# A two-layer decoder step: the first half's output projection inside the second half's attention, and smaller first chunks in three feed forwards

## The chip, the cores and the metric

The kernel runs on one core of a Trainium2 chip, as one program in one launch. The metric is the device time of that launch in microseconds (us). Five engines take part, each with its own queue that is worked off in order: TensorE (PE in the profile, with its weight loads as PEld), VectorE (DVE), ScalarE (ACT), GpSimd (POOL) and SyncE (SP, which issues nearly all DMAs).

## What is computed

One inference step of a decoder of two layers, in float32, with a model width of 1024, for 512 tokens of a prompt and 8 x 4 new tokens of other sequences. Cut to what matters here:

```python
for l in range(2):
    x = x + swiglu_half(x, ffn1_norm[l], ffn1_w_gu[l], ffn1_w_down[l])
    h = rmsnorm(x, mix_norm[l])
    # layer 0: gated linear attention; layer 1: sliding window of 128 with sinks
    q, k, v, ..., mq = split(h @ w_in)
    tok = gla_chunked(...) if l == 0 else swa_prompt(...)
    mo = mem_attention(mq, mem_k[l], mem_v[l])      # 256 memory tokens
    x = x + concatenate([tok, mo]) @ w_out
    x = x + swiglu_half(x, ffn2_norm[l], ffn2_w_gu[l], ffn2_w_down[l])
y = rmsnorm(x, final_norm)

def swiglu_half(x, g, w_gu, w_down):
    gate, up = split(rmsnorm(x, g) @ w_gu, 2)
    return 0.5 * ((silu(gate) * up) @ w_down)       # inner width 2816
```

## The kernel before

**Tiles.** The residual stream stands transposed, 8 tiles of 128 channels, in two halves of the tokens: half 0 has 288 columns (256 of the prompt and the 32 new ones), half 1 has 256. Every float32 matmul of the dense layers is made of three products in the fp32r type, high by high, high by low and low by high. So every weight and every activation is split into two parts: the high one by a copy on ACT (L298), the low one by a subtraction on DVE (L299). Names like `g6l`, `u1l`, `d7l`, `op7l` are the low parts of a gate, up, down or output projection weight block, those with `h` the high parts, those with `r` the block as loaded.

**A feed forward** has an inner width of 2816, 22 blocks of 128. `CHUNKS` cuts them into three chunks: 8, 7 and 7. Chunk 0 is done by `ffn` (L552) in a plain form for each half apart: per block a gate and an up product of 8 x 3 matmuls each, then the down projection of the chunk, 8 output tiles, each with 3 matmuls per block, whose sum is added to the residual tile (L580). Chunks 1 and 2 are done by `ffn_pair` (L498) for both halves at once, which stand beside each other in 272 columns: gate and up of the two halves are a product of 2 x 2 blocks, and it is computed with 7 products instead of 8, each of 12 matmuls. For this, sums and differences of the weights are formed per block in `quads` (L315; `s6s`, `t6s` are sums of block 6, `s6l` the low part of such a sum) and sums of the activations once per feed forward in `pair` (L443). `ffn_pair` opens each chunk with two matmuls that only open its two banks (L510).

**The order of a layer** is written in `layer` (L1259). A half goes through chunk 0 of its own; the joint chunks stand between: (1) chunk 0 of ffn1 for half 0, from the layer before or the start; (2) `enter_pair`, the norm and the joint forms, then the joint chunks (`both`); (3) chunk 0 of ffn1 for half 1 (`late`); (4) the norm and input projection of half 0 (`enter`, `project`); (5) attention of half 0, into which `weave` mixes what is left of `late`, the norm of half 1 and its input projection; (6) the output projection of half 0 (`out_proj`, L749; its residual adds are L755), with `hold` units of half 1's input projection kept back and put behind it, beside the norm for ffn2 (`enter`: `rstd` L394, whose sums over the channels are L404 on PE and whose scaling `r` is L410 on DVE, and `normed` L432); (7) attention of half 1, into which chunk 0 of ffn2 for half 0 is mixed; (8) the output projection of half 1; (9) `enter_pair` and the joint chunks of ffn2, beside the rest of chunk 0. In layer 0 the projection of the second layer's memory keys (`late_mem`) stands between (6) and (7).

A unit is a piece of a generator that ends at a `yield`: a gate or an up product of one block, an output tile of a projection, a step of an attention. `weave` (L1325) takes units of its two generators in proportion to the numbers that it is given. `FILL` holds for each layer how many units go ahead of the first weave (`lead`), are put just behind it (`pad`), are kept back (`hold`), come behind the second weave (`last`) and are kept for the entry of the joint chunks (`more`). `EARLY` is the number of units of chunk 0, two for each block and 8 for the down projection, 24.

In layer 1 the attention of the window (`swa_prompt`, L1125) works in groups of two heads: scores on PE (L1134), masks and sums on DVE (L1150 to L1170), transposes on PE (L1172), copies on DVE (L1176), values on PE (L1142). The order in which the engines' queues are filled comes from a scheduler with priorities: chunk ends ask for 6000 (`AHEAD`), the norms for 6500 (`SOON`), the attention in a weave for 3000 (`LEAD`). Dense matmuls of the plain form and all down and other projections are recorded at L356, those of `ffn_pair` at L342.

Of the kernel before, what the change touches and what calls it, by code (L numbers as in the profile page):

```python
# [30 lines left out]
SC = slice(2 * P, 2 * P + NS)  # L31
FF = 2816
FT = FF // P
CHUNKS = ((0, 8), (8, 15), (15, 22))
PW = (2 * P + NS + 2 * P) // 2
HK = KD // 2
EARLY = 2 * CHUNKS[0][1] + KD
MT = 256
GH, GK, GV = 4, 96, 192
LEVELS = (64, 32, 16, 8, 4, 2, 1)  # L40
# [128 lines left out]
def take(gen, n):  # L169
    for _ in range(n):  # L170
        if next(gen, StopIteration) is StopIteration:
            return
        yield


def drain(*gens):
    for g in gens:
        for _ in g:
            pass
# [53 lines left out]
class Build:  # L233
# [1 line left out]
    WB = (3, 4, 4, 2)  # L235
    MIX = 10
    FIRST, AHEAD, SOON, LEAD = 20000, 6000, 6500, 3000
    FILL = ((6, 1, 7, 2, 6), (7, 2, 5, 0, 9))
    HOMES = ((13, 8, 3), (8, 8, 3))

    def __init__(self, ctx, tc, d):
# [258 lines left out]
    def ffn_pair(self, tag, c, xs, gathered=()):  # L500


        nc = self.nc
        gu, dn = self.d["gu_" + tag], self.d["dn_" + tag]
        f0, f1 = CHUNKS[c]
        xa = [(h[:, :PW], l[:, :PW]) for h, l in xs[0]]
        xb, (t1, t2, t3, t4) = xs[1], xs["forms"]
        ga, gb = [], []
        for bank in self.pb.banks:
            nc.tensor.matmul(bank[:, :PW], xa[0][0][:, :P], xa[0][0], start=True, stop=True, skip_group_check=True)  # L510
        for f in range(f0, f1):
            w1, w2, s1, s2, s3, s4, w4 = self.quads(gu, f)
            pa, pc, pb = (b()[:, :PW] for b in (self.pac, self.pac, self.pb))
            c5, c2, act = (self.gas.u(PW) for _ in range(3))
            ahead = lambda: self.tc.high_priority(offset=self.AHEAD)
            self.product(pa, w1, xa[:HK], True)
            with ahead():
                nc.scalar.activation(pb, pa, AF.Copy)
            self.product(pc, s1, t1, True)
            self.product(pb, s2, t2, False)  # L520
            with ahead():
                nc.scalar.activation(c5, pc, AF.Copy)
            self.product(pa, w2, xa[HK:], False)
            with ahead():
                nc.scalar.activation(c2, pb, AF.Copy)
            self.product(pb, s3, t3, False)
            with ahead():
                nc.scalar.activation(act, pa, AF.Silu)
                nc.vector.tensor_tensor(out=c5, in0=c5, in1=pb, op=ALU.add)
            self.product(pc, s4, xb[HK:], False)  # L530
            self.product(pb, w4, t4, False)
            with ahead():
                nc.vector.tensor_tensor(out=c2, in0=c2, in1=pc, op=ALU.add)  # L533
                nc.scalar.activation(c2, c2, AF.Silu)  # L534
                nc.vector.tensor_tensor(out=act, in0=act, in1=pb, op=ALU.mult)
                ga.append(self.split(act, PW))
                nc.vector.tensor_tensor(out=c2, in0=c2, in1=c5, op=ALU.mult)  # L537
                gb.append(self.split(c2, PW))
            yield
        for m in range(KD):  # L540
            po = self.dense(dn[m, :, f0:f1, :], [ga, gb], f"d{m}")
            x0, x1 = self.x[0][m], self.x[1][m]
            with self.tc.high_priority(offset=self.AHEAD):
                for x, p in ((x0[:, :PW], po[0]), (x0[:, PW:], po[1][:, NH[1]:]), (x1, po[1][:, :NH[1]])):
                    nc.vector.scalar_tensor_tensor(out=x, in0=p, scalar=0.5, in1=x, op0=ALU.mult, op1=ALU.add)  # L545
            for h in gathered:
                self.stats((x0, x1)[h], h)
            if m == KD - 1:
                self.drop(ga, gb)
            yield  # L550

    def ffn(self, tag, c, halves, xs, gathered=(), tanh=False):  # L552
        nc = self.nc
        gu, dn = self.d["gu_" + tag], self.d["dn_" + tag]
        f0, f1 = CHUNKS[c]
        gs = {h: [] for h in halves}
        parts = [[(a[:, :NH[h]], b[:, :NH[h]]) for a, b in xs[h]] for h in halves]
        for f in range(f0, f1):
            pg = self.dense(gu[f], parts, f"g{f}")
            act = [self.gas.u(NH[h]) for h in halves]  # L560
            with self.tc.high_priority(offset=self.AHEAD):
                for a, p in zip(act, pg):
                    if tanh:
                        nc.scalar.activation(a, p, AF.Tanh, scale=0.5)
                        nc.vector.scalar_tensor_tensor(out=a, in0=a, scalar=1.0, in1=p, op0=ALU.add, op1=ALU.mult)
                    else:
                        nc.scalar.activation(a, p, AF.Silu)
            yield
            pu = self.dense(gu[FT + f], parts, f"u{f}")
            with self.tc.high_priority(offset=self.AHEAD):  # L570
                for h, a, p in zip(halves, act, pu):
                    nc.vector.tensor_tensor(out=a, in0=a, in1=p, op=ALU.mult)
                    gs[h].append(self.split(a, NH[h]))
            yield
        for m in range(KD):
            po = self.dense(dn[m, :, f0:f1, :], [gs[h] for h in halves], f"d{m}")
            for i, h in enumerate(halves):
                x = self.x[h][m]
                with self.tc.high_priority(offset=self.AHEAD):
                    nc.vector.scalar_tensor_tensor(out=x, in0=po[i], scalar=0.25 if tanh else 0.5, in1=x,  # L580
                                                   op0=ALU.mult, op1=ALU.add)
                if h in gathered:
                    self.stats(x, h)
            if m == KD - 1:
                self.drop([gs[h] for h in halves])
            yield
# [680 lines left out]
    def layer(self, l, project, attend, w_out, xs):  # L1267
# [16 lines left out]
            self.drop(r)  # L1284

        def both(tag, xs):
            drain(self.ffn_pair(tag, 1, xs), self.ffn_pair(tag, 2, xs, gathered=(0,)))
            self.drop(xs[0], self.extra)

        lead, pad, hold, last, more = self.FILL[l]  # L1290
        both(f1, xs)
        late = self.ffn(f1, 0, (1,), xs, gathered=(1,), tanh=True)
        mix[0] = enter(0, f"mix_{l}")
# [6 lines left out]
            mix[1] = enter(1, f"mix_{l}")  # L1300
            yield from project(1, mix[1], s[1])

        fill, units = second(), EARLY - lead + (22 if l == 0 else 8) - hold - pad
        self.weave(attend(0, s[0]), (take(fill, units), units))
        drain(take(fill, pad))
        self.drop(s[0].q if l else [])
        drain(self.out_proj(w_out, s[0].toks + s[0].mo, 0))
        out[0] = enter(0, f"ffn2_{l}")
        drain(fill)
        if l == 0:  # L1310
            drain(self.late_mem())
        early = self.ffn(f2, 0, (0,), out, tanh=True)
        more += last
        self.weave(attend(1, s[1]), (take(early, EARLY - more), EARLY - more))
        drain(take(early, last))
        self.drop(s[1].q if l else [])
        drain(self.out_proj(w_out, s[1].toks + s[1].mo, 1))
# [188 lines left out]
```

## Time and profile before

| what | us |
|---|---|
| time, median of 3 runs | 2153.05 |
| lowest and highest of these | 2150.55, 2155.71 |
| the profiled execution: device time | 2148.32 |
| the profiled execution: span of the core | 2146.5 |
| TensorE busy in the span | 2065.4 |
| VectorE busy in the span | 1539.5 |
| ScalarE busy in the span | 1067.2 |

The span runs from the first to the last instruction that the profile shows, and the device time lies 1.8 us above it. Busy times are sums over the instructions of an engine, so two engines that are busy at the same time both count. The mean clock that TensorE was granted is 0.983 of full speed. Where a row has several times, the first is the start in the span, the second the length.

### The profile page before, as it was taken

The numbers are of one execution on the slowest core, as the hardware profiler recorded it, in microseconds if no ns is written. First come the engines' busy times: TensorE is split into PE (matmuls) and PEld (weight loads), VectorE is DVE, ScalarE is ACT, GpSimd is POOL, SyncE is SP. The second block draws the span as 40 slices with busy tenths as digits, with TensorE's granted clock in tenths as the row PEclk, the third lists the DMA queues.
The fourth block names the chain that finished last, engine by engine and source line by source line (L and its number), as shares of the span: only waits on it lengthen the run. The fifth ranks groups of instructions, "written<-read, shape, count | busy, mean of one in ns | idle before, by whom it ended". The sixth has DMA issues, their size and how long they took to land.

```text
span 2146.5 us, 41032 instructions
## 1 busy us (share of the span) xinstructions
PE 2065.4 (96%) x16428; PEld 2000.7 (93%) x16428; DVE 1539.5 (72%) x3234; ACT 1067.2 (50%) x2089; POOL 35.8 (2%) x69
## 2 busy tenths in 40 slices
PE   6999999999999998999999999999998999999998
PEld 6999999998799998999999999999986988999998
DVE  7876675576668869757587776665877877966655
ACT  5554444754646645535355553444544544544434
POOL 5000000000000000000000000000000000000000
PEclk9999999999999999999999999999998999999999
DMA  7533253434454342323354523243443434232344
GB/s 230 157 115 109 79 156 118 138 120 148 152 160 159 125 143 79 108 87 103 113 178 142 177 89 114 74 148 122 151 147 105 143 109 128 89 109 79 110 149 128
DMA packets 90496, 273.03 MB, mean 127 GB/s; under 512 B 11408, under 2 KB 25248, under 8 KB 90272
## 3 DMA queue, kind: packets, MB, share of 16 engines
q1 hardware_dynamic: 89728, 269.87, 39.8%
q8 instruction: 129, 2.11, 0.4%
q14 instruction: 63, 0.52, 0.1%
q10 hardware_dynamic: 576, 0.52, 0.1%
HBM read 264.04 MB, written 7.70 MB: 127 GB/s over the span
## 4 chain that ended last, share of the span: by engine, by line
PE 85%; DVE 8%; DMA 4%; ACT 2%; issue 2%; SPq 0%; DVEq 0%; ACTq 0%
PE bank L356 55%; PE bank L342 21%; PE bank L904 1%; PE bank L1142 1%; DVE u L299 1%; PE bank L1134 1%; DMA u19r<-gu_ffn 0%; PE bank L649 0%; DMA u21r<-gu_ffn 0%; DMA u20r<-gu_ffn 0%; PE bank L705 0%; PE bank L416 0%; PE bank L679 0%; PE bank L1030 0%; PE bank L668 0%
## 5 line engine op out<-in xcount | busy, mean ns | idle before, releaser
L298 ACT ACTIVATE u<-u 128x272 fp32r<-128x272 f32 (+3 forms) x328 | 134.0, 422 | 132.5 <-DVE u L537 55.2
L545 DVE SCALAR_TENSOR_TENSOR x<-bank,x 128x16 f32<-128x16 f32 (+2 forms) x192 | 59.7, 342 | 115.0 <-PE bank L356 114.2
L299 DVE TENSOR_TENSOR u<-u,u 128x272 fp32r<-128x272 f32 (+3 forms) x328 | 137.2, 429 | 3.0 <-ACT u L298 1.2
L356 PE MATMUL bank<-u,d0h 128*128 128x272 f32 (+2 forms) x352 | 71.3, 289 | 0.0
L356 PE MATMUL bank<-u,d1h 128*128 128x272 f32 (+2 forms) x352 | 70.3, 288 | 0.0
L356 PE MATMUL bank<-u,d2h 128*128 128x272 f32 (+2 forms) x352 | 68.6, 289 | 0.4 <-DVE x L755 0.4
L356 PE MATMUL bank<-u,d3h 128*128 128x272 f32 (+2 forms) x352 | 68.0, 290 | 0.0
L356 PE MATMUL bank<-u,d4h 128*128 128x272 f32 (+2 forms) x352 | 67.5, 289 | 0.0
L356 PE MATMUL bank<-u,d5h 128*128 128x272 f32 (+2 forms) x352 | 67.3, 289 | 0.0
L356 PE MATMUL bank<-u,d6h 128*128 128x272 f32 (+2 forms) x352 | 67.1, 288 | 0.0
L356 PE MATMUL bank<-u,d7h 128*128 128x272 f32 (+2 forms) x352 | 67.0, 288 | 0.0
L534 ACT ACTIVATE u<-u 128x272 f32<-128x272 f32 x56 | 24.1, 430 | 73.2 <-DVE u L533 73.2
L356 PEld LDWEIGHTS bank<-u,d0h 128*128 128x128 f32 x352 | 56.3, 188 | 0.2
L356 PEld LDWEIGHTS bank<-u,d2h 128*128 128x128 f32 x352 | 55.4, 188 | 0.9 <-issue 0.5
L356 PEld LDWEIGHTS bank<-u,d1h 128*128 128x128 f32 x352 | 56.1, 188 | 0.0
L356 PEld LDWEIGHTS bank<-u,d3h 128*128 128x128 f32 x352 | 55.3, 188 | 0.3 <-DVE x L580 0.3
L356 PEld LDWEIGHTS bank<-u,d4h 128*128 128x128 f32 x352 | 55.4, 188 | 0.0
L356 PEld LDWEIGHTS bank<-u,d5h 128*128 128x128 f32 x352 | 55.2, 188 | 0.1
L356 PEld LDWEIGHTS bank<-u,d6h 128*128 128x128 f32 x352 | 55.2, 188 | 0.0
L356 PEld LDWEIGHTS bank<-u,d7h 128*128 128x128 f32 x352 | 55.1, 188 | 0.1
L356 PE MATMUL bank<-u,d2l 128*128 128x272 f32 (+2 forms) x176 | 51.0, 290 | 0.0
L356 PE MATMUL bank<-u,d4l 128*128 128x272 f32 (+2 forms) x176 | 50.9, 289 | 0.0
(1178 smaller groups left out, 7664.7 us busy)
## 6 DMA issues: line engine op xcount, KB each, us to landing
g0r<-gu_ffn SPq DMA_DIRECT2D x8, 512.0 KB, 3.5
u0r<-gu_ffn SPq DMA_DIRECT2D x8, 512.0 KB, 3.4
g1r<-gu_ffn SPq DMA_DIRECT2D x8, 512.0 KB, 3.4
u1r<-gu_ffn SPq DMA_DIRECT2D x8, 512.0 KB, 3.5
g2r<-gu_ffn SPq DMA_DIRECT2D x8, 512.0 KB, 3.4
u2r<-gu_ffn SPq DMA_DIRECT2D x8, 512.0 KB, 3.9
g3r<-gu_ffn SPq DMA_DIRECT2D x8, 512.0 KB, 3.5
u3r<-gu_ffn SPq DMA_DIRECT2D x8, 512.0 KB, 3.6
```

Of the source, the lines that this page charges most:

```text
L298: nc.scalar.activation(h, src, AF.Copy)
L299: nc.vector.tensor_tensor(out=l, in0=src, in1=h.bitcast(F32), op=ALU.subtract)
L342: self.nc.tensor.matmul(ps, a[:, k, :], x, start=start and k == 0 and j == 0, stop=k == len(xs) - 1 and j == 2, skip_group_check=True)
L356: self.nc.tensor.matmul(ps, w[:, k, :], x, start=i == 0 and j == 0, stop=i == kc - 1 and j == 2)
L534: nc.scalar.activation(c2, c2, AF.Silu)
L545: nc.vector.scalar_tensor_tensor(out=x, in0=p, scalar=0.5, in1=x, op0=ALU.mult, op1=ALU.add)
L904: nc.tensor.matmul(pv[:, c * half:(c + 1) * half], lhs[:, c * P:(c + 1) * P], second(rhs[:, c * P:(c + 1) * P]), start=True, stop=True)
L1134: nc.tensor.matmul(ps[:, e, P * (1 - back):][:, :P], q[j][64 * half:64 * half + 64, cols], self.keys(kv, half, n - back), start=True, stop ...
L1142: nc.tensor.matmul(dst, self.vt[n - i][:, 64 * kv:64 * kv + 64], pt[i].rearrange("p g t -> p (g t)"), start=i == 0, stop=i == last)
```

## The change

It has two parts.

**Chunks.** `CHUNKS` becomes a table with a row for each feed forward. ffn1_1 keeps 8, 7 and 7 blocks; ffn1_0, ffn2_0 and ffn2_1 get four chunks, 6, 6, 5 and 5. So in these three, two blocks more go from the plain to the joint form, and there is one joint chunk more. `EARLY` is 20 for them.

**Weave.** The kept back units of half 1's input projection (`hold`) now follow the first attention at once, ahead of the output projection of half 0; `pad` is gone. The output projection, the norm behind it and chunk 0 of ffn2 (in layer 0 with `late_mem` ahead) become one generator, `third`, which is mixed into the attention of half 1. `FILL` has other numbers.

```diff
-CHUNKS = ((0, 8), (8, 15), (15, 22))
+SMALL, LARGE = ((0, 6), (6, 12), (12, 17), (17, 22)), ((0, 8), (8, 15), (15, 22))
+CHUNKS = {"ffn1_0": SMALL, "ffn2_0": SMALL, "ffn1_1": LARGE, "ffn2_1": SMALL}
-EARLY = 2 * CHUNKS[0][1] + KD
+EARLY = {tag: 2 * c[0][1] + KD for tag, c in CHUNKS.items()}
-    FILL = ((6, 1, 7, 2, 6), (7, 2, 5, 0, 9))
+    FILL = ((6, 8, 2, 8), (7, 5, 0, 10))
...
         def both(tag, xs):
-            drain(self.ffn_pair(tag, 1, xs), self.ffn_pair(tag, 2, xs, gathered=(0,)))
+            last = len(CHUNKS[tag]) - 1
+            drain(*(self.ffn_pair(tag, c, xs, gathered=(0,) if c == last else ()) for c in range(1, last + 1)))
...
-        lead, pad, hold, last, more = self.FILL[l]
+        lead, hold, last, more = self.FILL[l]
...
-        fill, units = second(), EARLY - lead + (22 if l == 0 else 8) - hold - pad
+        fill, units = second(), EARLY[f1] - lead + (22 if l == 0 else 8) - hold
         self.weave(attend(0, s[0]), (take(fill, units), units))
-        drain(take(fill, pad))
+        drain(fill)
         self.drop(s[0].q if l else [])
-        drain(self.out_proj(w_out, s[0].toks + s[0].mo, 0))
-        out[0] = enter(0, f"ffn2_{l}")
-        drain(fill)
-        if l == 0:
-            drain(self.late_mem())
-        early = self.ffn(f2, 0, (0,), out, tanh=True)
-        more += last
-        self.weave(attend(1, s[1]), (take(early, EARLY - more), EARLY - more))
+
+        def third():
+            if l == 0:
+                yield from self.late_mem()
+            yield from self.out_proj(w_out, s[0].toks + s[0].mo, 0)
+            out[0] = enter(0, f"ffn2_{l}")
+            yield from self.ffn(f2, 0, (0,), out, tanh=True)
+
+        early, units = third(), EARLY[f2] + KD + (6 if l == 0 else 0) - more - last
+        self.weave(attend(1, s[1]), (take(early, units), units))
```

In the changed kernel a line of code beyond the first stands one line lower (L299 is L300, L755 is L756).

How the queues change is shown at three places. The first is DVE's queue at the entry of the joint chunks of ffn1 in layer 0, where the last joint forms of the activations (`u_825`, `u_829`, of `pair`) and the first weight sums (`s8s`, `t8s`) are made. Before:

```order
L299 TENSOR_TENSOR u_825<-u_694,u_824 128x272
L299 TENSOR_TENSOR d6l<-d6r,d6h 128x1024
L299 TENSOR_TENSOR u_829<-u_695,u_828 128x272
L580 SCALAR_TENSOR_TENSOR x_117<-bank_68,x_117 128x288
L299 TENSOR_TENSOR d7l<-d7r,d7h 128x1024
L580 SCALAR_TENSOR_TENSOR x_119<-bank_69,x_119 128x288
L299 TENSOR_TENSOR g8l<-g8r,g8h 128x1024
L327 TENSOR_TENSOR s8s<-u8r 128x512
L330 TENSOR_TENSOR t8s<-g8r,u8r 128x512
L580 SCALAR_TENSOR_TENSOR x_121<-bank_67,x_121 128x288
L328 TENSOR_TENSOR s8s<-s8s,g8r 128x512
```

DVE at the same place in the changed kernel, where the first joint block is block 6:

```order
L300 TENSOR_TENSOR g6l<-g6r,g6h 128x1024
L328 TENSOR_TENSOR s6s<-u6r 128x512
L331 TENSOR_TENSOR t6s<-g6r,u6r 128x512
L481 TENSOR_TENSOR u_695<-u_695,u_331 128x272
L300 TENSOR_TENSOR u_825<-u_694,u_824 128x272
L581 SCALAR_TENSOR_TENSOR x_123<-bank_67,x_123 128x288
L581 SCALAR_TENSOR_TENSOR x_125<-bank_68,x_125 128x288
L329 TENSOR_TENSOR s6s<-s6s,g6r 128x512
L300 TENSOR_TENSOR u_829<-u_695,u_828 128x272
L332 TENSOR_TENSOR t6s<-g6r,s6s 128x512
L300 TENSOR_TENSOR s6l<-s6s,s6h 128x1024
```

The weight sums of the first joint block now stand among the last forms of `pair`, ahead of `u_825` and `u_829`, and all residual adds of chunk 0 (`x_123`, `x_125` are the last two) stand ahead of `s6l`; before, two of them stood further back.

The second place is DVE in layer 1 from the last residual add of half 0's output projection (`x_125`) on. `bmq0l` and `bmq1l` are weight blocks of half 1's input projection, L1046 to L1048 its rotary embedding, `r` the scaling of the norm's sums. Before:

```order
L755 TENSOR_TENSOR x_125<-x_125,bank_69 128x288
L299 TENSOR_TENSOR bmq0l<-bmq0r,bmq0h 128x1024
L1046 STREAM_SHUFFLE u_20187<-bank_69 128x256
L1047 TENSOR_TENSOR u_20188<-bank_69,u_19697 128x256
L1048 TENSOR_TENSOR u_20187<-u_20187,u_19699 128x256
L410 TENSOR_SCALAR r<-bank_67 128x2
```

In the changed kernel DVE's rows from the same add on begin so (L1156 to L1171 are masks and softmax of half 1's attention):

```order
L756 TENSOR_TENSOR x_125<-x_125,bank_69 128x288
L300 TENSOR_TENSOR u1l<-u1r,u1h 128x1024
L300 TENSOR_TENSOR u_20118<-bank_72,u_20117 128x128
L1156 COPY_PREDICATED bank_71<-masks,bank_71 128x2x128
L300 TENSOR_TENSOR u_20120<-bank_72,u_20119 128x128
L1156 COPY_PREDICATED bank_70<-masks,bank_70 128x2x128
L300 TENSOR_TENSOR u_20122<-bank_72,u_20121 128x128
L1159 TENSOR_REDUCE wx<-bank_70 128x2
```

DVE's queue in the changed kernel reaches the scaling `r` with these rows, the last two of which are the 41st and 42nd behind the add:

```order
L1162 TENSOR_SCALAR wx<-wx 128x2
L1169 RECIPROCAL ws<-ws 128x2
L1171 TENSOR_SCALAR u_20676<-u_20676,ws 128x128 x2
L411 TENSOR_SCALAR r<-bank_67 128x2
L411 TENSOR_SCALAR r<-bank_67 32x1
```

Before, weight splits and rotary steps of half 1's input projection stood between the add and `r`, 5 rows; in the changed kernel 40 rows stand there, most of them softmax steps of half 1's attention.

The third place is PE's queue in layer 1, behind the last matmuls of half 0's output projection (`op7`). `bq3` is a weight block of half 1's input projection; L404 are the norm's sums. Before:

```order
L356 MATMUL bank_69<-u_18167,op7h 128x288
L356 MATMUL bank_69<-u_18168,op7h 128x288
L356 MATMUL bank_69<-u_18167,op7l 128x288
L404 MATMUL bank_67<-ones,u_19843 128x1
L356 MATMUL bank_69<-u_19651,bq3h 128x256
L356 MATMUL bank_69<-u_19652,bq3h 128x256
```

PE's queue in the changed kernel behind the same matmuls:

```order
L357 MATMUL bank_69<-u_18293,op7h 128x288
L357 MATMUL bank_69<-u_18294,op7h 128x288
L357 MATMUL bank_69<-u_18293,op7l 128x288
L1143 MATMUL bank_72<-u_20372,vt 64x256
L1143 MATMUL bank_72<-u_20350,vt 64x256
L1143 MATMUL bank_72<-u_20373,vt 64x256
L1143 MATMUL bank_72<-u_20351,vt 64x256
L1135 MATMUL bank_71<-u_13762,u_20042 128x128
```

PE's queue goes on so for 52 rows, of scores, transposes and values of half 1's attention, the norm's sums (L405), the spreading of `r` (L417) and transposes of the memory attention (L669), and comes then to the first gate product of ffn2 (`g0`):

```order
L1135 MATMUL bank_70<-u_14293,u_19931 128x128
L669 MATMUL bank_73<-c_ident,u_20872 128x128 x2
L669 MATMUL bank_73<-c_ident,u_20873 128x128 x2
L669 MATMUL bank_74<-c_ident,u_20883 128x128 x2
L669 MATMUL bank_74<-c_ident,u_20884 128x128 x2
L357 MATMUL bank_69<-u_20740,g0h 128x288
```

Before, dense products of half 1's input projection stood between `op7` and ffn2; now they stand ahead of `op0`, and only attention and norm stand between.

More of the change, by code (lines that the diff above doesn't have):

```diff
@@ L504, in ffn_pair @@
         gu, dn = self.d["gu_" + tag], self.d["dn_" + tag]
-        f0, f1 = CHUNKS[c]
+        f0, f1 = CHUNKS[tag][c]
         xa = [(h[:, :PW], l[:, :PW]) for h, l in xs[0]]
@@ L554, in ffn @@
         gu, dn = self.d["gu_" + tag], self.d["dn_" + tag]
-        f0, f1 = CHUNKS[c]
+        f0, f1 = CHUNKS[tag][c]
         gs = {h: [] for h in halves}
```

## The prediction

> **What bounds the kernel now.** The page comes first, for the busy shares and the chain that ended last.
>
> ```profile
> PE 2065.4 (96%) x16428; PEld 2000.7 (93%) x16428; DVE 1539.5 (72%) x3234; ACT 1067.2 (50%) x2089; POOL 35.8 (2%) x69
> PE 85%; DVE 8%; DMA 4%; ACT 2%; issue 2%; SPq 0%; DVEq 0%; ACTq 0%
> ```
>
> TensorE (PE) is busy for 96% of the span, and 85% of the last chain is its work. So matmuls taken out should pay, as long as nothing else decides at that place. The windows by stage say where that holds; their columns are the length, then busy time and instructions of PE, weight load, DVE, ACT and POOL, then granted clock and DMA.
>
> ```profile
> 118.00:351.00 233.00, 232.57 (x1851) 232.13 (x1849) 155.68 (x264) 103.27 (x178) 2.41 (x3) 1.00 0.36 111
> 390.00:616.00 226.00, 220.85 (x1850) 196.00 (x1849) 157.00 (x399) 134.81 (x308) 2.22 (x9) 0.99 0.45 142
> 616.00:660.00 44.00, 41.56 (x326) 40.91 (x325) 25.15 (x44) 21.78 (x36) 0.00 (x0) 1.00 0.52 163
> 660.00:797.00 137.00, 134.47 (x1078) 132.09 (x1076) 113.18 (x304) 81.65 (x195) 1.43 (x7) 1.00 0.42 135
> 797.00:835.00 38.00, 32.01 (x216) 30.78 (x216) 32.70 (x73) 17.97 (x36) 0.00 (x0) 0.91 0.31 102
> 1600.00:1637.00 37.00, 25.94 (x263) 16.58 (x264) 19.54 (x89) 9.42 (x42) 0.00 (x0) 0.68 0.34 105
> 1637.00:1792.00 155.00, 148.50 (x1189) 138.63 (x1186) 124.37 (x338) 81.25 (x199) 0.10 (x1) 0.99 0.39 124
> 1792.00:1835.00 43.00, 37.97 (x273) 36.82 (x273) 36.52 (x83) 23.22 (x41) 0.00 (x0) 0.96 0.34 107
> ```
>
> In the joint chunks of a feed forward (118 to 351) PE has no hole at all. In the attention of both halves (390 to 616, 616 to 797, 1637 to 1792) it lacks 2 to 5% only, since the feed forward's units fill it. Holes stand where a chain of small steps has no such filler beside it: 37 us at 1600, and the two entries into `ffn_pair` for ffn2 (797 to 835 and 1792 to 1835), where DVE is busy for 32.7 of 38 and 36.5 of 43 us: there DVE decides.
>
> **Part 1: six blocks change their form.** The chain of waits has long stretches of each kind of matmul (start, us, what, records):
>
> ```profile
> 66.43 35.30 PE bank L356 x268
> 117.78 70.66 PE bank L342 x564
> 1093.69 50.55 PE bank L356 x420
> ```
>
> That is 0.1317 us for a matmul of 288 columns, 0.1253 for 272 in `ffn_pair`, 0.1204 for 256. In the plain form a block has 48 matmuls for each half, so 6.32 + 5.78 = 12.10 us; in the joint form 84, so 10.52. Six blocks (two in each of ffn1_0, ffn2_0, ffn2_1) save 9.5 us. Three more chunks bring two opening matmuls each, 6 x 0.125 = 0.75. **PE's work shrinks by 8.7 us.** The down projections keep their matmuls. What three more chunks add elsewhere I cost at nothing: 24 smaller weight loads against 12 that go, 62 more residual updates and short adds on DVE, seven more table loads on ACT. In the joint stage they lie beside PE (DVE 155.7 and ACT 103.3 of 233 us). Without that cover three chunk ends might cost 2 us.
>
> **Part 2: the entry of ffn1_0.** Chunk 0 of half 0 runs while DVE prepares the joint forms (`pair`). Two blocks and the smaller down projection take 2 x 6.32 + 48 x 0.1317 = 19.0 us of cover away. PE began the joint chunk at 117.8; it would now be at the first `g6` products at 98.8, and 3.0 us later, at 101.8, at the first `s6`. Is DVE ready?
>
> ```profile
> 70.00:80.00 10.00, 10.00 (x78) 10.00 (x78) 10.00 (x24) 6.16 (x12) 0.00 (x0) 1.00 0.20 62
> 80.00:90.00 10.00, 10.00 (x78) 10.00 (x78) 10.00 (x20) 5.37 (x11) 0.00 (x0) 1.00 0.76 215
> 90.00:100.00 10.00, 10.00 (x78) 10.00 (x78) 9.88 (x23) 5.17 (x12) 0.00 (x0) 1.00 0.66 197
> 100.00:110.00 10.00, 9.97 (x76) 9.74 (x75) 7.33 (x12) 4.99 (x7) 0.00 (x0) 1.00 0.45 156
> 66.88 0.49 DVE L452 SCALAR_TENSOR_TENSOR u<-x,gains,u 128x256 f32<-128x256 f32 x1 [1.27 <-ACT u L421]
> 115.37 1.23 DVE L299 TENSOR_TENSOR s8l<-s8s,s8h 128x1024 fp32r<-128x1024 f32 x1 [0.48 <-ACT s8h L298]
> 116.51 0.45 DVE L580 SCALAR_TENSOR_TENSOR x<-bank,x 128x288 f32<-128x288 f32 x1
> ```
>
> DVE is full from 70 to 100 us. From the first row of `pair` (66.88) to the end of `s8l` (116.60) pass 49.7 us. By the new order the same stretch, to `s6l`, loses 12 weight splits of 128x1024 (1.14 us each, from 115.37 to 116.51), two products and two splits of activations, and gains eight splits of 128x768 (three quarters in size, some 0.9) and two residual updates: with 0.45 for a short row, 13.7 - 7.2 + 1.8 - 0.9 = 7.4 us less. So `s6l` ends at 109.2, or at 105.5 if the 3.7 us in which DVE stood idle there close up. PE waits 3.7 to 7.4 us; I take **+5**, nearer to a DVE that stays full.
>
> **Part 3: the entries of ffn2.**
>
> ```profile
> 1805.88 3.25 DVE L452 SCALAR_TENSOR_TENSOR u<-x,gains,u 128x256 f32<-128x256 f32 x8
> 1831.22 1.22 DVE L299 TENSOR_TENSOR s8l<-s8s,s8h 128x1024 fp32r<-128x1024 f32 x1
> ```
>
> In layer 1, PE waits until 1832.4 for `s8l`, 26.6 us behind the first row of `pair`. In the new order three wide splits fewer, four of 128x768, one activation split, three subtractions and two updates more stand ahead of `s6l`: -3.4 + 3.6 + 0.4 + 1.1 + 0.9 = 2.6, say 2.3 us later. And PE comes sooner: behind the second output projection it has two products and eight down units of 18 matmuls (25.3 us) where it had one and eight of 24 (28.4), so 3.1 less. Together 5.4. In layer 0 the cover is equal (8 x 18 for 6 x 24 matmuls), and only the second block's sums come later, by three 0.6 us rows: 1.6. **+7** for both.
>
> **Part 4: the weave.** The output projection leaves a place where it ran alone; its 8 units now fill the second attention. The holes of that stretch may close: 44 - 41.6 and 137 - 134.5 in layer 0, 155 - 148.5 in layer 1, so 5.0 + 6.5. What takes their place is the norm behind the projection (`enter`, `rstd`, `normed`), which had the held units beside it.
>
> ```profile
> 647.90 0.45 DVE L755 TENSOR_TENSOR x<-x,bank 128x288 f32<-128x288 f32 x1
> 659.91 0.94 DVE L438 SCALAR_TENSOR_TENSOR u<-x,gains,u 128x288 f32<-128x288 f32 x2
> 1673.76 0.46 DVE L755 TENSOR_TENSOR x<-x,bank 128x288 f32<-128x288 f32 x1 [0.61 <-PE bank L356]
> 1689.14 0.94 DVE L438 SCALAR_TENSOR_TENSOR u<-x,gains,u 128x288 f32<-128x288 f32 x2
> 1763.47 1.94 PE L1142 MATMUL bank<-u,vt 128*64 128x256 f32 x8 [0.60 <-DVE u L1176]
> 1765.35 1.91 PE L1134 MATMUL bank<-u,u 64*128 64x128 f32 x16
> 1771.57 0.38 PE L1172 MATMUL bank<-c_ident,u 128*128 128x128 f32 x2
> 1773.37 0.43 PE L1172 MATMUL bank<-c_ident,u 128*128 128x128 f32 x2
> 1774.32 1.08 PE L1142 MATMUL bank<-u,vt 128*64 128x256 f32 x8 [0.52 <-DVE u L1176]
> ```
>
> From the last residual add to the first normed row pass 12.0 us in layer 0 and 15.4 in layer 1; held projections filled them. In layer 1 the new DVE order puts the middle rows of two softmax groups between that add and the sums' scaling (`r`), and PE finds nothing but these groups between `op7` and `g0`. One group without other work takes 10.85 us (1763.47 to 1774.32), in which PE has 1.94 + 1.91 + 0.38 + 0.43 = 4.7 of its own: 6.2 idle, so 12.4 for two, less about 1 for the sums' matmuls: +11.5, against 6.5 that go. In layer 0 no such wait stands ahead of `r`; shorter DVE work leaves some 11 us from `op7` to `g0`, about half filled by attention: +5 against 5.0. **+5** for both; from -6, if the groups' steps are done early, to +13, if the old holes stay. Queued behind the waiting `r` on DVE are the masks of the third group, and behind those PE's next values. Late next is attention, but it ends inside `g4`, with filler left.
>
> Layer 0's first attention has 17 us less filler (4 x 24 and 8 x 6 matmuls of 256). PE was full there (220.9 of 226) and DVE had 157, so it can shrink: nothing; +17 if it can't.
>
> **Part 5: the clock.**
>
> ```profile
> 1595.00:1600.00 5.00, 5.00 (x58) 4.40 (x58) 3.41 (x10) 3.00 (x10) 0.00 (x0) 0.97 0.39 114
> 1600.00:1605.00 5.00, 3.96 (x29) 3.30 (x30) 2.12 (x16) 1.29 (x10) 0.00 (x0) 0.50 0.21 84
> 1615.00:1620.00 5.00, 2.06 (x18) 1.04 (x14) 4.31 (x20) 2.47 (x12) 0.00 (x0) 1.00 0.51 157
> ```
>
> PE's granted clock falls to a half in holes and the dense work behind them starts slow: 0.91 over the 38 us from 797 is 6.8 us at half rate, some 3 us lost. Three pauses are new (two in part 4, one in part 2) and one goes: I add **+2**, from 0 to 6.
>
> [...]
>
> **The sum.** -8.7 + 5 + 7 + 5 + 2 = +10.3 us. Against the profiled execution (2148.3 us, span 2146.5) that is 2158.6; the median shown is 2153.05, 4.7 above it, and I forecast beside the median: 2163.
>
> **Rivals.** (a) DVE is early enough and PE's saving comes through. Its place is DVE's queue at the three entries and behind `op7`; it decides if the first row of `pair` comes some 5 us sooner than 66.9, and a softmax group alone takes under 8 us and not 10.85. Then part 2 gives 1.5, part 3 two, part 4 -6, the clock 1: -10.2, 2143. For it: DVE has 3.7 us of idle in its stretch. Against: three windows at 10 of 10. (b) The weave closes its holes (-6) but both kinds of entry wait as worked out (5 + 7 + 1): -1.7, 2151. (c) Layer 0's attention does not shorten, and 12 of the 17 us are lost on top: 2175. Against it speaks DVE at 157 of 226. That the change does nothing of what it says is excluded by the order of the built program.
>
> **How the numbers follow.** Forecast 0.45 (its own range 2157 to 2170), (a) 0.32, (b) 0.14, (c) 0.09. 0.2% (4.3 us) is about what a measurement of this kernel can tell from no change: faster 0.32, same 0.14, slower 0.54. For 8 in 10 the range takes in half of (a), all of (b) and half of (c): 2143 to 2178.
>
> **What would show it.** A PE hole of about 5 us at 100 to 110, ended by `s6l`; longer waits on `s6` at both ffn2 entries; in layer 1 some 27 us between the last `op7` and the first `g0` without a dense matmul, with the clock at a half in it. If PE is busy there, or `s6l` lands before 102, the forecast is wrong and (a) holds. If layer 0's first attention keeps its 226 us, (c) does.

## The result and the profile after

The changed kernel takes 2157.55 us (median of 20 runs, 2153.39 to 2161.91), the kernel before 2152.86 (20 runs): a ratio of 1.0023, with an interval from 1.0015 to 1.0032. It is slower by some 4.7 us, where 10 had been forecast. The profiled executions differ alike: spans of 2151.7 and 2146.5 us.

The page of the changed kernel, busy time by engine and the chain that ended last:

```profile
PE 2065.9 (96%) x16362; PEld 1998.1 (93%) x16362; DVE 1569.9 (73%) x3356; ACT 1082.0 (50%) x2138; POOL 35.5 (2%) x69
PE 88%; DVE 7%; ACT 3%; DMA 1%; issue 1%; DVEq 0%; SPq 0%; ACTq 0%
```

PE is as busy as before with 66 instructions fewer. Matmuls took longer in places (the mean granted clock is 0.976 here and was 0.983 before), so the busy time does not show the saved ones. The windows by stage do show where PE waits (columns as in the prediction):

```profile
60.00:115.00 55.00, 52.29 (x387) 50.68 (x387) 49.74 (x107) 31.47 (x59) 0.00 (x0) 1.00 0.38 118
410.00:660.00 250.00, 246.28 (x2080) 222.95 (x2079) 189.28 (x519) 159.32 (x379) 3.50 (x15) 0.98 0.46 145
660.00:697.00 37.00, 37.00 (x295) 35.90 (x293) 27.90 (x74) 18.63 (x42) 0.00 (x0) 1.00 0.37 123
697.00:709.00 12.00, 8.00 (x42) 7.12 (x41) 8.97 (x30) 9.72 (x29) 0.10 (x1) 0.74 0.28 94
709.00:777.00 68.00, 68.00 (x536) 67.60 (x536) 48.97 (x100) 36.38 (x72) 0.00 (x0) 1.00 0.42 134
777.00:815.00 38.00, 32.26 (x237) 30.82 (x236) 34.19 (x76) 20.46 (x39) 0.00 (x0) 1.00 0.31 101
1634.00:1692.00 58.00, 57.62 (x472) 54.94 (x472) 48.88 (x133) 30.87 (x75) 0.10 (x1) 0.99 0.39 128
1692.00:1722.00 30.00, 18.04 (x108) 12.48 (x107) 19.17 (x76) 12.65 (x42) 0.10 (x1) 0.62 0.10 36
1722.00:1783.00 61.00, 60.40 (x488) 58.48 (x487) 47.23 (x117) 32.20 (x73) 0.00 (x0) 0.99 0.40 132
1783.00:1824.00 41.00, 35.22 (x244) 33.16 (x243) 35.15 (x83) 23.00 (x43) 0.00 (x0) 0.96 0.34 100
```

The old holes of the second attention are closed in both layers (37.00 of 37, 68.00 of 68, 57.62 of 58, 60.40 of 61). Two new ones stand behind `op7`: 12 us in layer 0 (697), 30 us in layer 1 (1692), the second at a clock of 0.62.

An account by stages shows what the shares hide. The boundaries are the starts of the first gate product (`g0`) of a chunk 0 in the two traces, and at the end the start of the last matmul. "Matmuls" is the change in dense work, by the count of matmuls and the prediction's 0.1317, 0.1253 and 0.1204 us; the remainder is what is left of the change in length: PE's waits, and matmuls that took longer.

| from | before us | after us | length changes | matmuls | remainder |
|---|---|---|---|---|---|
| start to ffn1_0 of half 1 | 0 to 351.1 | 0 to 370.4 | +19.3 | +14.3 | **+5.0** |
| to ffn2_0 of half 1 (layer 0's attentions, ffn2's entry) | to 1062.3 | to 1074.4 | -7.2 | -3.0 | **-4.2** |
| to ffn1_1 of half 0 | to 1149.1 | to 1145.7 | -15.5 | -17.3 | +1.8 |
| to ffn1_1 of half 1 | to 1473.9 | to 1471.2 | +0.7 | 0 | +0.7 |
| to ffn2_1 of half 1 (layer 1's attentions, ffn2's entry) | to 2064.7 | to 2087.2 | +25.2 | +14.3 | **+10.9** |
| to the end | to 2140.1 | to 2145.5 | -17.1 | -17.3 | +0.2 |

The matmuls save 9.0, the remainders cost 14.4; by the pages PE's idle time grew by 4.7 of these. Layer 1 and the stage of ffn1_0 are near the forecast; layer 0 gained where a small loss had been forecast. Each row rests on one trace of each kernel, and that matters in layer 0: of the runs below, `e6_more6`, `e9_more9` and `e12_ratio` have the code of the changed kernel there, and the same account of their traces gives layer 0's two attentions (up to the end of the second output projection) -3.4, -0.8 and +4.5, where the changed kernel has -3.0. So no gain is shown in layer 0's attentions. The other stages of layer 0 agree better (+5.0 to +6.3 in the first row).

### The profile page after: what moved, and what is told of

Read it like the earlier page. It is cut to its first block, busy times and chain, and to the rows that moved or that the text cites. A ratio compares the mean times of both kernels' runs of the same rounds, so it can differ in the third digit from the quotient of the medians.

```text
span 2151.7 us, 41119 instructions
## 1 busy us (share of the span) xinstructions
PE 2065.9 (96%) x16362; PEld 1998.1 (93%) x16362; DVE 1569.9 (73%) x3356; ACT 1082.0 (50%) x2138; POOL 35.5 (2%) x69
## 4 chain that ended last, share of the span: by engine, by line
PE 88%; DVE 7%; ACT 3%; DMA 1%; issue 1%; DVEq 0%; SPq 0%; ACTq 0%
PE bank L357 51%; PE bank L343 28%; PE bank L905 1%; PE bank L1143 1%; PE bank L1135 1%; DVE u L300 1%; PE bank L417 0%; PE bank L706 0%; PE bank L669 0%; PE bank L680 0%; PE bank L405 0%; PE bank L650 0%; DVE x L581 0%; PE bank L1031 0%; PE bank L1173 0%
## 5 line engine op out<-in xcount | busy, mean ns | idle before, releaser
L299 ACT ACTIVATE u<-u 128x272 fp32r<-128x272 f32 (+3 forms) x328 | 133.3, 421 | 94.4 <-DVE u L538 43.7
L546 DVE SCALAR_TENSOR_TENSOR x<-bank,x 128x16 f32<-128x16 f32 (+2 forms) x264 | 81.0, 342 | 95.5 <-PE bank L357 94.3
L300 DVE TENSOR_TENSOR u<-u,u 128x272 fp32r<-128x272 f32 (+3 forms) x328 | 137.8, 431 | 9.3 <-ACT u L299 8.0
L536 DVE TENSOR_TENSOR u<-u,bank 128x272 f32<-128x272 f32 x62 | 26.8, 433 | 36.9 <-PE bank L343 36.9
L530 DVE TENSOR_TENSOR u<-u,bank 128x272 f32<-128x272 f32 x62 | 27.1, 437 | 35.6 <-PE bank L343 35.1
```

The source lines that it names most:

```text
L299: nc.scalar.activation(h, src, AF.Copy)
L300: nc.vector.tensor_tensor(out=l, in0=src, in1=h.bitcast(F32), op=ALU.subtract)
```

## The experiments

All ratios are to the kernel before, from runs on the same chip, with their 95% intervals. Where nothing else is said, a diff is against the changed kernel, and it is cut to the lines that matter.

**First, the two parts of the change apart.** The theory was that the stages add up: 5 us at ffn1_0's entry, 10 in layer 1's new order, a small gain in layer 0's. The rival was the account of the prediction. `e1_chunks` has the chunk table in the old order (its diff is against the kernel before):

```diff
-CHUNKS = ((0, 8), (8, 15), (15, 22))
+CHUNKS = {"ffn1_0": SMALL, "ffn2_0": SMALL, "ffn1_1": LARGE, "ffn2_1": SMALL}
-    FILL = ((6, 1, 7, 2, 6), (7, 2, 5, 0, 9))
+    FILL = ((6, 1, 7, 2, 8), (7, 2, 5, 0, 10))
```

> The old order of a layer, with the new chunks in ffn1_0, ffn2_0 and ffn2_1 (the units kept for the ffn2 entries as in the changed kernel: 8 and 10). Theory A, the account by stages of the two traces (PE work -8.7, entry of ffn1_0 +5.2, entries of ffn2 +1): -2.5 us against before, 2150.4, a ratio of 0.9988. Theory B, the account of the prediction (entries of ffn2 +7): +3 to +4, 2156 to 2157, a ratio of 1.0015 or more.

Measured: 1.0055 (1.004 to 1.007), 2162.34 us, slower than the whole change. Both theories fell; the second had the sign, but 3 to 4 us of a loss of 11. `e2_weave` has the new order with the old chunks:

```diff
-CHUNKS = {"ffn1_0": SMALL, "ffn2_0": SMALL, "ffn1_1": LARGE, "ffn2_1": SMALL}
+CHUNKS = {"ffn1_0": LARGE, "ffn2_0": LARGE, "ffn1_1": LARGE, "ffn2_1": LARGE}
-    FILL = ((6, 8, 2, 8), (7, 5, 0, 10))
+    FILL = ((6, 8, 2, 6), (7, 5, 0, 9))
```

> The new order of a layer with the old chunks of 8, 7 and 7 blocks everywhere. Theory A (layer 0's stretch -3, layer 1's stretch +10, up to +1.7 behind layer 0): +7 to +9 us against before, 2160 to 2162, with a hole of about 30 us behind the last op7 of half 0 in layer 1. Theory B (layer 0's stretch nothing, layer 1's +5, clock +1.5): +6.5, 2159.5; and if the hole is not what costs, about 2153.

Measured: 0.9971 (0.9961 to 0.9981), 2144.28 us. The new order alone is faster, by 6 us. Both theories fell again, and the trace says where: the hole behind `op7` in layer 1 is there, but half as long as in the changed kernel (windows of the run with the new order alone):

```profile
1696.00:1712.00 16.00, 10.53 (x71) 7.39 (x72) 11.64 (x45) 7.90 (x24) 0.00 (x0) 0.65 0.21 67
```

**ffn1_0 back, and layer 1's order back.** `e3_ffn1_large`:

```diff
-CHUNKS = {"ffn1_0": SMALL, "ffn2_0": SMALL, "ffn1_1": LARGE, "ffn2_1": SMALL}
+CHUNKS = {"ffn1_0": LARGE, "ffn2_0": SMALL, "ffn1_1": LARGE, "ffn2_1": SMALL}
```

> The changed kernel with ffn1_0 back at 8, 7 and 7 blocks. If the shorter cover at its entry costs 5.2 us and its two blocks save 2.9 (a third of 8.7), undoing it gains 2.3: 2155.3. Rival: the small holes from 88 to 114 us have another cause (a late weight block, whose DMA waits in any case): they stay, and 2.9 us are lost: 2160.4. PE's wait in 60 to 120 us should be under 1 us by the first and about 3.6 by the second.

Measured: 1.0031 (1.0018 to 1.0044), no different from the changed kernel (1.0015 to 1.0032). PE's wait at the entry is gone, as the first theory had it: in the 60 us from 60 to 120, PE is busy for 59.69, and for 57.29 in the changed kernel. So the wait comes from the smaller chunk, and what the entry costs and what the two blocks save cancel within the noise. `e4_l1_old` keeps layer 0 as changed and gives layer 1 its old order:

```diff
-    FILL = ((6, 8, 2, 8), (7, 5, 0, 10))
+    FILL = ((6, 0, 8, 2, 8), (7, 2, 5, 0, 10))
...
+        if l == 1:
+            drain(self.out_proj(w_out, s[0].toks + s[0].mo, 0))
+            out[0] = enter(0, f"ffn2_{l}")
+            drain(fill)
```

> The changed kernel with the old order in layer 1 alone (held units of half 1's projection behind half 0's output projection, beside the norm; feed forward alone woven into attention 1). Theory A (layer 1's stretch from 1637 to 1792 us lost 10.3): 2147.2, a ratio to before of 0.997 to 0.998, and no stretch over 15 us without a dense matmul behind op7. Theory B (it lost 5 only): 2152.5. Rival C, the hole only moves to another place of the attention: 2157.

Measured: 1.0018 (1.0008 to 1.0027), nearly the changed kernel's. Against `e1_chunks`, which differs in layer 0's order alone, it is 0.0037 faster: with small chunks the new order gains 8 us in layer 0. That layer 1's new order as such costs 10 was wrong: with small chunks the old order there is as slow. Why small chunks cost as much in the old order was not settled.

**A new theory: how many softmax groups stand ahead of `r`.** The 30 us hole of the changed kernel: PE in order of time, without some rows of scores and transposes, and the row of DVE that scales `r`:

```profile
1692.26 1.08 PE L1143 MATMUL bank<-u,vt 128*64 128x256 f32 x8
1694.88 1.04 PE L405 MATMUL bank<-ones,u 128*128 128x1 f32 x10
1699.00 0.43 PE L1173 MATMUL bank<-c_ident,u 128*128 128x128 f32 x2 [3.08 <-DVE u L1171]
1700.63 0.66 PE L1173 MATMUL bank<-c_ident,u 128*128 128x128 f32 x2 [1.21 <-DVE u L1171]
1701.81 1.98 PE L1143 MATMUL bank<-u,vt 128*64 128x256 f32 x8 [0.52 <-DVE u L1177]
1709.41 0.66 PE L1173 MATMUL bank<-c_ident,u 128*128 128x128 f32 x2 [3.61 <-DVE u L1171]
1713.04 0.66 PE L1173 MATMUL bank<-c_ident,u 128*128 128x128 f32 x2 [2.97 <-DVE u L1171]
1714.29 1.98 PE L1143 MATMUL bank<-u,vt 128*64 128x256 f32 x8 [0.59 <-DVE u L1177]
1718.19 1.78 PE L417 MATMUL bank<-u,ones 128*128 128x128 f32 x6
1722.25 0.59 PE L357 MATMUL bank<-u,g0h 128*128 128x288 f32 x1
1709.37 0.21 DVE L411 TENSOR_SCALAR r<-bank 128x2 f32<-128x2 f32 x2
```

The sums that `r` needs (L405) are done at 1695.9, but DVE comes to `r` at 1709.37 only, behind the softmax of a second group. In DVE's queue of the new order alone (`e2_weave`), 18 rows stand between the last add and `r`, in the changed kernel 40. The count follows from `weave`: it takes the generator with the least (units taken + 1) / units. The norm is written at the filler's 9th unit. With 18 units that is 9/18, at which 10 of the attention's 20 steps have been written (a tie goes to the attention); with 23 it is 9/23, and 7 have been. Two groups stand ahead with 10 steps, one with 7 to 9. By this theory (D in the expectations) it is not the block that is missing, but a count in `FILL` that makes the hole. Runs that move units and blocks apart can tell. `e5_ffn21_large` undoes ffn2_1 alone:

```diff
-CHUNKS = {"ffn1_0": SMALL, "ffn2_0": SMALL, "ffn1_1": LARGE, "ffn2_1": SMALL}
+CHUNKS = {"ffn1_0": SMALL, "ffn2_0": SMALL, "ffn1_1": LARGE, "ffn2_1": LARGE}
-    FILL = ((6, 8, 2, 8), (7, 5, 0, 10))
+    FILL = ((6, 8, 2, 8), (7, 5, 0, 9))
```

> The changed kernel with ffn2_1 alone back at 8, 7 and 7 blocks (9 units kept for its entry, as before). DVE's order then has one softmax group ahead of the scaling r in layer 1, not two. Theory D (the smaller chunk costs in layer 1's second attention, by the second group ahead of r): the stretch without dense work behind op7 falls from 30 to 16 us and the time to about 2145. Rival E (the chunks cost in layer 0, or evenly): 2153 to 2157.

Measured: 0.9974 (0.9964 to 0.9983), 2146.33 us. The loss of the changed kernel is thus in layer 1; this run changes both the chunk there and the units in the weave (23 for 18). `e6_more6` keeps that chunk small and moves units:

```diff
-    FILL = ((6, 8, 2, 8), (7, 5, 0, 10))
+    FILL = ((6, 8, 2, 8), (7, 5, 0, 6))
```

> The changed kernel with four units more of ffn2_1's first chunk in the weave of layer 1 (22 in place of 18) and four fewer, 9.5 us of matmuls, at the entry of its joint chunks. Blocks as in the changed kernel; one softmax group ahead of r. Theory D: the hole behind op7 falls to 16 us, 10 to 13 us are gained there and up to 9.5 lost at the entry: 2147 to 2157. Theory F (what counts is that two blocks of filler are gone, not their place): the attention's stretch stays as long, and the entry's loss comes on top: 2160 to 2167.

Measured: 0.9981 (0.9969 to 0.9992), 2146.98 us: no block came back, and 9 us did. `e7_ffn10_small` asks what ffn1_0 alone does in the new order (this diff and the next are against `e2_weave`):

```diff
-CHUNKS = {"ffn1_0": LARGE, "ffn2_0": LARGE, "ffn1_1": LARGE, "ffn2_1": LARGE}
+CHUNKS = {"ffn1_0": SMALL, "ffn2_0": LARGE, "ffn1_1": LARGE, "ffn2_1": LARGE}
```

> The new order with small chunks in ffn1_0 alone, against the new order with large ones (2144.3). If its entry costs 3.8 to 5.2 us and its blocks save 2.9: 2145 to 2147. Rival: its second chunk 0 is the filler of layer 0's first attention, and without it up to 17 us of cover are gone: 2150 to 2160.

Measured: 0.9972 (0.996 to 0.9983), the same as the new order alone. `e8_large_more14` makes the hole without taking a block:

```diff
-    FILL = ((6, 8, 2, 6), (7, 5, 0, 9))
+    FILL = ((6, 8, 2, 6), (7, 5, 0, 14))
```

> The new order with large chunks, and five units of ffn2_1's first chunk moved from the weave of layer 1 (18 in place of 23) to the entry of its joint chunks. All blocks are as in the new order with large chunks (2144.3); two softmax groups stand ahead of r. Theory D: the hole behind op7 grows from 16 to 30 us, and the time by 7 to 13: 2151 to 2157. Theory F: no block is gone, so 2144 to 2147.

Measured: 1.0019 (1.0008 to 1.0031), 0.0048 or 10 us above the new order alone. No block is gone, and the loss is back. Its windows show the 30 us hole of the changed kernel once more:

```profile
1697.00:1727.00 30.00, 17.88 (x109) 12.44 (x108) 18.91 (x76) 12.43 (x41) 0.10 (x1) 0.68 0.11 36
```

**The threshold, and the ratio by itself.** `e9_more9` changes one number, so that the weave has 19 units (9/19, 9 steps):

```diff
-    FILL = ((6, 8, 2, 8), (7, 5, 0, 10))
+    FILL = ((6, 8, 2, 8), (7, 5, 0, 9))
```

> The changed kernel with one number of FILL changed: 9 units kept for the entry of ffn2_1 in place of 10, so 19 and not 18 units in layer 1's weave. One softmax group stands ahead of r, not two. Theory D: the hole behind op7 falls from 30 to 16 us, 2157.5 to 2145 - 2148, at most 2.4 us lost at the entry. Theory F (cover by blocks): one unit changes nothing, 2156 to 2159.

Measured: 0.9976 (0.9966 to 0.9986), 0.0047 or 10 us below the changed kernel. PE behind `op7` in this run, cut in the same way, with DVE's row of `r`:

```profile
1693.19 1.08 PE L1143 MATMUL bank<-u,vt 128*64 128x256 f32 x8
1695.81 1.04 PE L405 MATMUL bank<-ones,u 128*128 128x1 f32 x10
1699.93 0.66 PE L1173 MATMUL bank<-c_ident,u 128*128 128x128 f32 x2 [3.07 <-DVE u L1171]
1702.88 0.66 PE L1173 MATMUL bank<-c_ident,u 128*128 128x128 f32 x2 [2.30 <-DVE r L429]
1703.65 1.78 PE L417 MATMUL bank<-u,ones 128*128 128x128 f32 x6
1705.36 1.98 PE L1143 MATMUL bank<-u,vt 128*64 128x256 f32 x8
1709.28 0.61 PE L357 MATMUL bank<-u,g0h 128*128 128x288 f32 x1
1699.89 0.21 DVE L411 TENSOR_SCALAR r<-bank 128x2 f32<-128x2 f32 x2
```

`r` is served behind one group, 6.9 us behind the projection's last matmul and not 17.3 as in the changed kernel; `g0` follows 16 us behind the projection. `e12_ratio` moves no unit at all, and only tells the weave another number of steps for half 1's attention:

```diff
-                           (chain(self.mem_prompt(1, s.mq, s.mo), *extra), 6 + 17 * (h == 0))), (37 if h == 0 else 20)
+                           (chain(self.mem_prompt(1, s.mq, s.mo), *extra), 6 + 17 * (h == 0))), (37 if h == 0 else 18)
```

> The changed kernel with no unit moved: only the number of steps that the weave is told for half 1's attention in layer 1 is 18 in place of 20, so that its steps are written later against the 18 units of the filler. One softmax group ahead of r. Theory D: the hole falls to 16 us with the entry as it was, 2145 to 2148. Rival (the units at the entry are what the run with 22 units gained by): 2157.

Measured: 0.9972 (0.996 to 0.9985), with a hole of 16 us (last `op7` at 1699.2, `g0` at 1715.5). The theory holds, and no rival fits all the runs: with 18 units against 20 steps the hole is 30 us and the ratio 1.0019 to 1.0031 (the changed kernel, `e3_ffn1_large`, `e8_large_more14`), and with one group less ahead of `r` the hole is 16 us and the ratio 0.9971 to 0.9981 (`e2_weave`, `e5_ffn21_large`, `e6_more6`, `e7_ffn10_small`, `e9_more9`, `e12_ratio`), with small chunks in ffn2_1 and with large ones. The order of writing costs 10 us, not the blocks.

**Two that gave nothing.** `e10_chunks_fill` is the old order with small chunks and as many units in the second weaves as before the change (the diff is against `e1_chunks`):

```diff
-    FILL = ((6, 1, 7, 2, 8), (7, 2, 5, 0, 10))
+    FILL = ((6, 1, 7, 2, 2), (7, 2, 5, 0, 5))
```

> The old order with the small chunks, as in the first run of the chunks alone (2162.3), but with as many units in the second weave of each layer as before the change: 16 in layer 0 (2 kept, not 8) and 15 in layer 1 (5 kept, not 10). If the chunks alone cost by a weave that ran out of units (its last output projection then waits 14.6 us for the attention's end in layer 0), 8 to 15 us come back in the attentions and up to 14 + 12 us of cover are gone at the entries: 2150 to 2165, with the stretch of half 1's output projection in layer 0 at 3 to 6 us without dense work. If the blocks themselves are missing there, that stretch stays at 14 us and the time rises to 2170 or more.

Measured: 1.0044 (1.0028 to 1.006), as slow as `e1_chunks` within the intervals. In the old order it does not matter whether the weave or the entry gets the remaining units; what the smaller chunks cost there stays, and its cause is open. The units only move the waits. In `e1_chunks` the weave of layer 0 has run out before the attention ends (its window at half 1's output projection, beside 37.93 of 39 us at the same place before):

```profile
737.00:787.00 50.00, 44.95 (x333) 42.31 (x331) 30.93 (x79) 23.98 (x64) 0.00 (x0) 0.93 0.29 89
```

In `e10_chunks_fill`, PE waits instead behind the second output projections, until the first sum is there: 10.0 us in layer 1, where `e1_chunks` has 5.9.

`e11_large_more6` (its diff is against `e2_weave`) has large chunks and 26 units in layer 1's weave (9/26, 6 steps):

```diff
-    FILL = ((6, 8, 2, 6), (7, 5, 0, 9))
+    FILL = ((6, 8, 2, 6), (7, 5, 0, 6))
```

> The new order with large chunks (2144.3) and three units more in layer 1's weave (26 in place of 23), three fewer at the entry of ffn2_1. In DVE's order no softmax group is left between the last residual add and r but the masks of one. Theory D: the hole behind op7 falls from 16 to some 8 us; the entry loses up to 9.5 us of cover, of which the run with 22 units lost 2: 2137 to 2142. Rival: the attention's steps that stood in the hole wait later, 2144 to 2150.

Measured: 0.997 (0.9958 to 0.9982), no better than the new order alone. The hole falls to 10.4 us (last `op7` at 1696.5, `g0` at 1706.9), but the total stays, as the rival had it. By the account of stages, layer 1's second attention with its output projection is only 1.8 us better than in `e2_weave`, though its hole is 6 us shorter, and behind that the smaller cover costs 1.3. That the missing group waits elsewhere in the attention fits this; at which place is open.

The fastest are thus the new order with large chunks (0.9971, 0.997) and with small ones and a ratio that leaves one group ahead of `r` (0.9972, 0.9976); their intervals overlap.

## Why the prediction was wrong in size

**Part 1** was right. Long stretches of each kind in the changed kernel's chain of waits:

```profile
66.74 10.02 PE bank L357 x76
113.65 49.90 PE bank L343 x396
```

That is 0.1318 us for a matmul of 288 columns and 0.1260 for 272, against 0.1317 and 0.1253 charged, and the counts changed as worked out. That six blocks pay nothing in the end is shown by the pair `e2_weave` and `e9_more9` (0.9971 and 0.9976): the saving of 0.4% is given back in full. By the account of stages the traces of these two differ, beyond the matmuls, by +4.4 up to the second half of ffn1_0 and by +6.9 behind the second output projections of both layers, so it is given back where chunks became smaller. With one trace each, and a scatter of a few us, the shares are rough.

**Part 2** (+5, a hole ended by `s6l`) had the right size for the stage, +5.0, and the wrong picture. In 60 to 115 us PE stands still for 2.7, in small pieces, of which these are some:

```profile
88.26 0.53 PE L357 MATMUL bank<-u,d3h 128*128 128x288 f32 x2 [0.72 <-DVE x L581]
104.37 0.77 PE L343 MATMUL bank<-fv,s6h 128*128 128x272 f32 x4 [0.20 <-ACT s6h L299]
105.63 0.39 PE L343 MATMUL bank<-fv,s6l 128*128 128x272 f32 x1 [0.49 <-DVE s6l L300]
113.65 0.52 PE L343 MATMUL bank<-fv,s7h 128*128 128x272 f32 x2 [0.25 <-ACT s7h L299]
```

`s6l` was there at 105.6, as by the lower end (105.5): DVE's idle 3.7 us did close up, but for 1.1. PE waited for it for 0.5 only. The other 2.3 of the stage's +5.0 are not idle time of this stretch; the prediction put what a further joint chunk adds at nothing, and the runs do not tell its price apart.

**Part 3** (+7 at the entries of ffn2) failed as a step. In layer 1 DVE reads so (the changed kernel):

```profile
1794.63 3.26 DVE L453 SCALAR_TENSOR_TENSOR u<-x,gains,u 128x256 f32<-128x256 f32 x8 [0.72 <-ACT u L422]
1822.18 1.22 DVE L300 TENSOR_TENSOR s6l<-s6s,s6h 128x1024 fp32r<-128x1024 f32 x1
```

From the first row of `pair` to the end of the weight sum pass 28.8 us, 2.2 more than before (2.3 forecast). But that first row now comes 11.3 us behind the output projection's last matmul (1783.3) and not 13.5, since two residual adds that waited for PE stand behind it now. The sum is ready 40.1 us behind the projection in both kernels, so this term of the wait is nothing. The other 3.1, the shorter cover, was charged as a wait of PE. In the 40.1 us up to the sum PE is idle for 5.8 us, where it had been 5.0, so 0.8 more; for the rest it was busy, at a clock of 0.96 in place of 0.99. In layer 0, 1.6 had been forecast for the sums of the second block. PE's wait behind the first sum did grow by that much (from 2.3 to 3.8 up to the next chunk 0), but up to the first sum it fell from 5.2 to 3.8, and the two cancel.

Nor is the time at which DVE has the sum ready fixed. In `e11_large_more6`, with three units less at this place, it is ready far sooner:

```profile
1813.19 3.25 DVE L453 SCALAR_TENSOR_TENSOR u<-x,gains,u 128x256 f32<-128x256 f32 x8
1823.49 1.21 DVE L300 TENSOR_TENSOR s8l<-s8s,s8h 128x1024 fp32r<-128x1024 f32 x1
```

That is 23.7 us behind the projection (1801.0) in place of 40. PE's idle time up to the sum is 5.0 us there, and 4.9 in `e2_weave`, which has the three units more: 9.5 us less cover, and no longer wait. The units that cover the entry bring splits and adds to DVE themselves, and the sum stands at another place of DVE's queue; that the scheduler puts it where it expects PE to ask for it is a guess. A full DVE in a trace was thus no proof of a bound here. The remainder from the projection's end to the last chunk 0 grew by 1.8 us in layer 1, and in layer 0 it fell by 1.0, so +1 in all. Other pairs of traces have more: from `e2_weave` to `e9_more9`, whose cover in layer 1 is a unit shorter, the two remainders grow by 6.9. But there, too, PE does not wait longer up to the sum in layer 1 (4.5, where `e2_weave` has 4.9); most of the loss lies behind it, and its cause is open.

**Part 4** (+5) named the right hole, gave it some 27 us and had 30.2; the two groups in it, 12.5 us apart (1701.81 to 1714.29, charged at 10.85), are what the trace shows. PE's idle time in it is 12.0 (30.00 less 18.04), where 11.5 had been charged. With the old holes closed, PE's idle time in the stretch from half 1's projection to the end of the second output projection rose from 6.5 to 12.9 by the windows, 6.4 where 5 had been forecast. By the account of stages that stretch (1637.6 to 1792.4 before, 1634.0 to 1783.3 after) lost 10.3; the other 4, by subtraction, are busy time. The rows of the hole show 1.8 of these at half clock in two sets of value matmuls (1.98 in place of 1.08 each); the rest I put down to the other attention matmuls there. Layer 0's two attentions came out 3 better, within the scatter. But the step gave the hole to the weave, and the runs show that it hangs on a tie of 10/20 and 9/18 in `FILL`: without it the same weave is 5 to 6 us faster than before the change.

**Part 5** (+2) put the price of the clock behind the holes. It lies in them:

```profile
1697.00:1702.00 5.00, 1.28 (x6) 0.78 (x8) 3.72 (x18) 1.91 (x10) 0.00 (x0) 0.75 0.02 10
1702.00:1707.00 5.00, 3.80 (x24) 2.37 (x22) 1.81 (x6) 0.56 (x2) 0.00 (x0) 0.50 0.00 0
1707.00:1712.00 5.00, 0.66 (x2) 0.31 (x2) 3.27 (x19) 4.20 (x13) 0.10 (x1) 0.50 0.00 0
1712.00:1717.00 5.00, 3.38 (x17) 1.89 (x19) 4.53 (x21) 2.52 (x9) 0.00 (x0) 0.50 0.00 0
1717.00:1722.00 5.00, 5.00 (x25) 4.26 (x24) 1.97 (x5) 1.08 (x3) 0.00 (x0) 0.50 0.01 3
1722.00:1727.00 5.00, 5.00 (x42) 4.67 (x41) 5.00 (x20) 4.22 (x16) 0.00 (x0) 0.86 0.00 0
```

A clock of 0.86 over the 5 us behind the hole is 1.4 us at half rate, so 0.7 lost. Inside, the clock is at 0.50 for 20 us (1702 to 1722), and the work in it, with PE busy for 12.8 of them, did not raise it; that is most of the 4 us of part 4, by an estimate from the attention's rows there (1.98 us in place of 1.08 for eight matmuls of L1143, twice, and 2.08 for 16 of L1135, where 12 took 0.94 at the hole's start). The half rate came behind a pause of 3.08 us (before 1699.00): the clock was 1.00 from 1697 to 1699 and 0.58 over the next 3 us. From 1714.29 on PE had no pause, and the clock was still at 0.50 up to 1722, 7.7 us later. Nor did every hole of the kernel before bring it down: from 1615 to 1620 the clock was 1.00, with PE busy for 2.06 of the 5 us. The +2 was charged for the dense work behind three new pauses, less one that goes; what the traces show is 0.7 us behind one hole and some 4 inside it.

So the sum was 5 too high, and one step accounts for it: the entries of ffn2 (part 3) came out at +1 in place of +7 (**the step that failed**), since PE's waits up to the first sums there grew by 0.8 only in layer 1 and shrank by 1.4 in layer 0. Part 1 gave -9.0 for -8.7 and part 2 +5.0 for +5. Parts 4 and 5 gave 7.3 for 7 together (-3.0 in layer 0's attentions, +10.3 in layer 1's), and that is luck: layer 1's is 5 more than charged, mostly by the clock inside the hole, and layer 0's is within the scatter of its traces. Another 1.3 lies in stages for which nothing was charged.

Rival (a) did not occur: `s6l` landed at 105.6 and not before 102. Rival (b), a weave that closes its holes, is nearest to what the same change gives with one number altered; with 0.9976 that is 5 us faster than before, where (b) had 1.7. Rival (c) did not occur: layer 0's two attentions together lost nothing that can be told from the scatter, with 17 us less filler.

## What to carry to other kernels

Where two streams are mixed by counts, look for what the counts place ahead of the one short chain that everything behind it waits for; a tie or one unit can move a whole group past it, and that is cheaper to correct than the work it is blamed on. Matmuls that are the cover of a latency chain need not be saved by making them fewer: six blocks in a cheaper form gained nothing here. Do the parts of a change apart before you explain their sum: one part gained 6 us, the other lost 11 on top of it, and the trace of both together pointed at the wrong one.

## What the runs showed of the hardware

In the 30 us hole of the changed kernel the lower clock makes the work longer: eight value matmuls of the attention (L1143) take 1.08 us at the hole's start, at a clock of 1.00, and 1.98 once it is 0.50. One group took 10.85 us before, from 1763.47, at a mean clock of 0.84 and not without other work, since PE was busy for 9.30 of them; the two in the hole, at a clock of 0.50 throughout, follow each other by 12.5. Twenty us with PE busy for 12.8, the last 7.7 of them without a pause, did not bring the clock back from 0.50; it was 0.86 over the next 5 us.
